# Gate and up in two passes, with 512-column and 256-column matmuls, in a decoder layer in fp32

## The chip, the cores and the metric

The kernel runs on one core of one Trainium2 chip. The metric is the time of one execution on the device, in microseconds (us), as the median of several runs. Engines are named as in the profile: PE is TensorE (PEld its weight loads), DVE is VectorE, ACT is ScalarE, POOL is GpSimd, SP is the engine that issues most DMAs.

## What is computed

One decoder layer on 512 tokens of width 2048 in fp32: a mixer (convolution beside attention), then a gated FFN of width 5632. Only the first half of the FFN is touched:

```python
h = rmsnorm(x, norm2_g[l])
x = x + (jax.nn.silu(h @ w_gate[l]) * (h @ w_up[l])) @ w_down[l]
```

## The kernel before

**Products in three parts.** An fp32 operand is kept as a rounded upper half (hi) and the rest (lo), and a product is three matmuls that accumulate in one PSUM bank: hi x hi, hi x lo, lo x hi. The weights are the stationary operand, the activations the moving one.

**Seven products for eight.** Gate and up take a scheme of the Strassen kind. A block is 256 features of the input by 512 tokens, cut in 2 x 2 quadrants (128 features by 256 tokens); weights are cut in 2 x 2 quadrants of 128 x 128. Seven products of sums of quadrants stand for eight. `block_sums` (L591 on) makes the seven sums of each of the eight blocks (j = 0 to 7) once, with hi in columns 0 to 255 and lo in 256 to 511 of one tile: blocks 0 to 3 in slots b16 to b43, blocks 4 to 7 in slots a0 to a13 and a16 to a29.

**Steps.** The work is a list of steps, one chunk of weights (512 KB) each. In `gu_group` (L661) a step is one block j with 256 columns of gate and the same of up: seven products, each for gate (i = 0) and up (i = 1), of three matmuls of 256 columns (L676 to L678), 42 in all. Eight steps are a pair, 22 pairs make 176 steps. Gate fills columns 0 to 255 and up columns 256 to 511 of a product's bank, seven banks per pair, taken in turn from a ring of eight.

**Splitting a chunk.** `split_gu` (L622) runs two steps ahead, loads run three ahead. The chunk has four quadrants of 256 columns. Three are used as they are, 768 columns: ACT casts them to hi (wh, L638), DVE subtracts to get lo (wl, L649). The four sums are made by DVE (t13, t24: L639, L645, L646), cast by ACT (L647, L648) and subtracted by DVE (L650, L651). raw, wh and wl have three buffers each, t13 and t24 two, their halves three.

**Earlier steps** use another way to get lo, `split_add` (L195): ACT writes the negated hi to wl (L198), and a DMA on POOL's queue adds the weights from memory (L199).

**After a pair** `gu_post` (L683) copies or adds the seven banks into SBUF and puts the remaining sums, the row scale, Silu and the product into a background list, from which each step takes as much as its credit allows. The result, two tiles of hid per pair, goes to memory on POOL's queue (L709).

**Around the stage.** At its entry the last blocks are still being made, and the row scale of the norm (L159, L139, L148, L149) is computed. At its exit `reload_hid` (L741) brings 14 tiles of hid back, on POOL's queue, into the slots of blocks 0 to 3, and `split_hid` makes halves of them; w_down follows, whose first accumulators are banks 0 to 3. A scheduler sets each engine's order from the program and the credits; each engine then works its own instructions in order.

Of the kernel before, what the change touches and what calls it, by code (L numbers as in the profile page):

```python
# [16 lines left out]
P = 128  # L17
S = 512
# [19 lines left out]
STEP_US, GU_STEP_US = 4.6, 5.0  # L38
# [8 lines left out]
def decoder_layer(ctx: ExitStack, tc, xT, w_in, w_out, w_gu, w_dn, par, lamv, out):  # L47
# [543 lines left out]
    def block_sums(j):  # L591
        h = [slotB(44 + i) for i in range(2)]
        for i in range(2):
            kt = 2 * j + i
            nc.scalar.activation(h[i], xres[kt], AF.Copy, scale=pp[:, C_G2 + kt : C_G2 + kt + 1])
        s13, s24 = slotB(46), slotB(47)
        t1, t2 = slice(0, HS), slice(HS, S)
        nc.vector.tensor_tensor(s13[:, t1], h[0][:, t2], h[1][:, t2], op=ALU.add)
        nc.vector.tensor_tensor(s24[:, t1], s13[:, t1], h[0][:, t1], op=ALU.subtract)
        nc.vector.tensor_tensor(s13[:, t2], h[0][:, t2], h[0][:, t1], op=ALU.subtract)  # L600
        nc.vector.tensor_tensor(s24[:, t2], h[1][:, t1], s24[:, t1], op=ALU.subtract)
        forms = [
            h[0][:, t1], h[1][:, t1], s24[:, t2], h[1][:, t2], s13[:, t1], s24[:, t1], s13[:, t2],
        ]
        blocks[j] = []
        for m, f in enumerate(forms):
            t = block_slot(j, m)
            split(t[:, t1], t[:, t2], f)
            blocks[j].append((t[:, t1], t[:, t2]))
# [14 lines left out]
    def split_gu(t, src):  # L624
# [4 lines left out]
        credit[0] -= 3.4  # L629
# [7 lines left out]
        pure = slice(256, 1024)  # L637
        nc.scalar.copy(wh[:, pure], t[:, pure])  # L638
# [10 lines left out]
        nc.vector.tensor_tensor(wl[:, pure], t[:, pure], r32(wh[:, pure]), op=ALU.subtract)  # L649
# [9 lines left out]
    ORDER = [0, 1, 5, 6, 4, 2, 3]  # L659

    def gu_group(pair):  # L661

        accs = {}
        for j in range(NJ):

            def run(q, j=j):
                for n, m in enumerate(ORDER):
                    if j == 0:
                        accs[m] = bank(RING[(7 * pair + n) % 8])
                    sh, sl = blocks[j][m]  # L670
                    qh, ql = q[m]
                    for i in range(2):
                        acc = accs[m][:, i * HS : (i + 1) * HS]
                        cut = slice(i * P, (i + 1) * P)
                        first, last = j == 0 and i == 0, j == NJ - 1 and i == 1
                        nc.tensor.matmul(acc, lhsT=qh[:, cut], rhs=sh, start=first, stop=False)  # L676
                        nc.tensor.matmul(acc, lhsT=qh[:, cut], rhs=sl, start=False, stop=False)  # L677
                        nc.tensor.matmul(acc, lhsT=ql[:, cut], rhs=sh, start=False, stop=last)  # L678

            post = (lambda: gu_post(pair, [accs[m] for m in range(7)])) if j == NJ - 1 else None  # L680
            steps.append((w_gu[pair, j], run, post, split_gu))

    def gu_post(pair, accs):  # L683
        m1, m2, m3, m4, m5, m6, m7 = accs
        tt = nc.vector.tensor_tensor
        u2, c22, v3, v4 = slotA(14, F32), slotA(15, F32), slotA(30, F32), slotA(31, F32)
        c11, u3 = slotB(44), slotB(45)
        nc.scalar.copy(u2, m1)
        tt(c11, m2, u2, op=ALU.add)
        nc.scalar.copy(c22, m5)  # L690
        tt(u2, m6, u2, op=ALU.add)
        nc.scalar.copy(v3, m3)
        tt(u3, m7, u2, op=ALU.add)  # L693
        nc.scalar.copy(v4, m4)
        hid = [slotB(46 + f) for f in range(2)]

        def finish(c, f, i):

            r = rB[1][:, i * HS : (i + 1) * HS]

            def norm():
                c3 = c.rearrange("p (k t) -> p k t", k=2)
                tt(c3, c3, r.unsqueeze(1).to_broadcast([P, 2, HS]), op=ALU.mult)
                nc.scalar.activation(c[:, :HS], c[:, :HS], AF.Silu)

            def product():
                tt(hid[f][:, i * HS : (i + 1) * HS], c[:, :HS], c[:, HS:], op=ALU.mult)
                if i == 1:
                    nc.gpsimd.dma_start(hid_kept[2 * pair + f], hid[f])  # L709

            return norm, product

        n11, p11 = finish(c11, 0, 0)
        n12, p12 = finish(u2, 1, 0)
        n21, p21 = finish(u3, 0, 1)
        n22, p22 = finish(c22, 1, 1)
        bg.extend(
            [
                (0.6, n11),
                (0.6, lambda: tt(u2, u2, c22, op=ALU.add)),  # L720
                (0.6, lambda: tt(c22, u3, c22, op=ALU.add)),
                (0.6, lambda: tt(u2, u2, v3, op=ALU.add)),
                (0.6, lambda: tt(u3, u3, v4, op=ALU.subtract)),
                (0.3, p11),
                (0.6, n12), (0.6, n22), (0.6, n21),
                (0.3, p12), (0.3, p22), (0.3, p21),
            ]
        )
# [61 lines left out]
    for pair in range(NPAIR):  # L790
        gu_group(pair)
# [233 lines left out]
def _layout(i):  # L1025
# [19 lines left out]
    gu = np.stack([f["w_gate"][0], f["w_up"][0]], axis=1).reshape(NJ, 2, P, 2, NPAIR, 2, P)  # L1045
    gu = gu[:, :, :, :, :, ::-1].transpose(4, 0, 2, 1, 5, 3, 6).reshape(NPAIR, NJ, P, 1024)
# [44 lines left out]
```

## Time and profile before

| | us |
|---|---|
| median of 3 runs (2079.77 to 2082.02) | 2081.11 |
| the profiled execution | 2081.82 |
| its span, first to last instruction | 2079.9 |
| PE busy in the span | 2054.6 |
| DVE busy | 1460.8 |
| ACT busy | 942.1 |
| POOL busy | 194.1 |

The mean granted TensorE clock is 0.997 of full speed. Busy times overlap between engines. PE durations overlap too, since matmuls are pipelined: how often they start is read from the timeline. An instruction that issues a DMA is listed with its engine; the transfer itself lands later.

### The profile page before, as it was taken

To read this page: it belongs to the slowest core of one execution; us is meant where nothing else is said; L and a number is where in the kernel's file an instruction comes from. 1 tells how busy PE (TensorE), PEld (TensorE's weight loads), DVE (VectorE), ACT (ScalarE), POOL (GpSimd) and SP (SyncE) were. 2 spreads that over 40 slices of the span, in tenths; PEclk is the share of its full clock that TensorE was granted. 3 is DMA by queue.
4 is the path that set the end of the run, shared out by engine and by line. 5 is a ranking of instruction groups with operands and counts; after the bars stand their busy time and mean duration, and the time that the engine had idled before them with its cause. 6 is when DMAs were issued, how large, how long until landed. Compare 5 with 4: busy or idle time off the path is not lost.

```text
span 2079.9 us, 33053 instructions
## 1 busy us (share of the span) xinstructions
PE 2054.6 (99%) x12852; PEld 1855.1 (89%) x12852; DVE 1460.8 (70%) x2624; ACT 942.1 (45%) x1541; POOL 194.1 (9%) x268
## 2 busy tenths in 40 slices
PE   8999999999999999999999999999999999999997
PEld 6888887888888999999999999999998888888887
DVE  7899935678635899888888988988886333332244
ACT  5433447677744554444444444444444222221232
POOL 5111111111110000000000000000013000000004
PEclk9999999999999999999999999999999999999998
DMA  6888887677763334333333333333358334323232
GB/s 209 186 187 196 191 188 158 149 166 185 181 167 113 122 106 139 112 113 122 122 109 106 132 113 121 120 115 112 113 167 309 102 124 139 98 95 101 92 112 81
DMA packets 84205, 289.74 MB, mean 139 GB/s; under 512 B 10193, under 2 KB 10705, under 8 KB 84049
## 3 DMA queue, kind: packets, MB, share of 16 engines
q1 hardware_dynamic: 61776, 210.04, 30.9%
q0 software_dynamic: 22272, 77.61, 17.3%
q8 instruction: 100, 1.64, 0.3%
q14 instruction: 57, 0.46, 0.1%
HBM read 267.68 MB, written 19.92 MB: 138 GB/s over the span
## 4 chain that ended last, share of the span: by engine, by line
PE 85%; issue 7%; DVE 3%; POOL 1%; ACT 1%; DMA 1%; SPq 0%; DVEq 0%; POOLq 0%; ACTq 0%
PE k L206 14%; PE k L207 14%; PE k L205 14%; PE k L676 14%; PE k L677 14%; PE k L678 14%; POOL wl L199 1%; PE k L519 1%; DMA raw<-w_gu_dram 0%; DVE a L288 0%; PE k L470 0%; DMA wl<-w_v_dram 0%; PE k L469 0%; DVE b L445 0%; PE k L508 0%
## 5 line engine op out<-in xcount | busy, mean ns | idle before, releaser
L205 PE MATMUL k<-a,wh 128*128 128x512 f32 (+1 forms) x992 | 385.4, 389 | 3.2 <-ACT wh L178 1.8
L207 PE MATMUL k<-a,wl 128*128 128x512 f32 (+1 forms) x992 | 383.7, 387 | 2.7 <-DVE wl L179 2.4
L206 PE MATMUL k<-a,wh 128*128 128x512 f32 (+1 forms) x992 | 384.5, 388 | 1.6 <-DVE a L288 1.5
L179 DVE TENSOR_TENSOR wl<-raw,wh 128x1024 fp32r<-128x1024 f32 (+1 forms) x108 | 134.3, 1244 | 319.0 <-ACT wh L178 319.0
L178 ACT CAST wh<-raw 128x1024 fp32r<-128x1024 f32 (+1 forms) x108 | 112.0, 1037 | 365.0 <-PE k L206 355.2
L647 ACT CAST b<-b 128x512 fp32r<-128x512 f32 x176 | 109.2, 621 | 268.4 <-PE k L677 232.1
L205 PEld LDWEIGHTS k<-a,wh 128*128 128x128 f32 x992 | 186.4, 188 | 41.8 <-ACT wh L178 2.4
L207 PEld LDWEIGHTS k<-a,wl 128*128 128x128 f32 x992 | 186.4, 188 | 41.1 <-DVE wl L179 3.7
L206 PEld LDWEIGHTS k<-a,wh 128*128 128x128 f32 x992 | 186.4, 188 | 39.7 <-DVE a L288 2.9
L676 PE MATMUL k<-b,b 128*128 128x256 f32 x704 | 200.2, 284 | 0.9 <-DVE b L693 0.7
L678 PE MATMUL k<-b,b 128*128 128x256 f32 x704 | 199.6, 283 | 0.0
L676 PE MATMUL k<-a,b 128*128 128x256 f32 x704 | 199.2, 283 | 0.0
L677 PE MATMUL k<-a,b 128*128 128x256 f32 x704 | 199.2, 283 | 0.0
L678 PE MATMUL k<-a,b 128*128 128x256 f32 x704 | 199.2, 283 | 0.0
L677 PE MATMUL k<-b,b 128*128 128x256 f32 x704 | 199.2, 283 | 0.0
L335 DVE SCALAR_TENSOR_TENSOR b<-b,pp,b 128x511 f32<-128x511 f32 (+14 forms) x240 | 176.6, 736 | 8.1
L639 DVE TENSOR_TENSOR b<-raw 128x512 f32<-128x512 f32 x176 | 119.7, 689 | 79.8 <-DMA raw<-w_gu_dram 78.6
L205 PE MATMUL k<-b,wh 128*128 128x512 f32 x448 | 174.3, 389 | 0.0
L206 PE MATMUL k<-b,wh 128*128 128x512 f32 x448 | 174.3, 389 | 0.0
L207 PE MATMUL k<-b,wl 128*128 128x512 f32 x448 | 174.3, 389 | 0.0
L649 DVE TENSOR_TENSOR wl<-raw,wh 128x768 fp32r<-128x768 f32 x176 | 167.5, 952 | 0.2 <-ACT wh L638 0.2
L648 ACT CAST b<-b 128x512 fp32r<-128x512 f32 x176 | 109.1, 620 | 120.2 <-DVE b L646 95.8
(212 smaller groups left out, 4961.0 us busy)
## 6 DMA issues: line engine op xcount, KB each, us to landing
raw<-w_gu_dram SPq DMA_DIRECT2D x176, 512.0 KB, 3.3
raw<-w_down_dram SPq DMA_DIRECT2D x88, 512.0 KB, 3.3
raw<-w_qk_dram SPq DMA_DIRECT2D x32, 512.0 KB, 5.5
wl<-w_qk_dram POOLq DMA_DIRECT2D x32, 512.0 KB, 7.4
raw<-w_out_dram SPq DMA_DIRECT2D x32, 512.0 KB, 3.9
raw<-w_conv_dram SPq DMA_DIRECT2D x30, 512.0 KB, 5.2
wl<-w_conv_dram POOLq DMA_DIRECT2D x24, 512.0 KB, 7.7
hid<-b POOLq DMA_DIRECT2D x44, 256.0 KB, 3.3
```

Source lines behind the costliest of these rows:

```text
L178: nc.scalar.copy(hi, src)
L179: nc.vector.tensor_tensor(lo, src, r32(hi), op=ALU.subtract)
L205: nc.tensor.matmul(acc, lhsT=ah, rhs=bh, start=first, stop=False)
L206: nc.tensor.matmul(acc, lhsT=ah, rhs=bl, start=False, stop=False)
L207: nc.tensor.matmul(acc, lhsT=al, rhs=bh, start=False, stop=last)
L335: nc.vector.scalar_tensor_tensor(c[:, d:], h[:, : S - d], w, c[:, d:], op0=ALU.mult, op1=ALU.add)
L639: nc.vector.tensor_tensor(t13.rearrange("p (i c) -> p i c", i=2), t[:, a].unsqueeze(1).to_broadcast([P, 2, 256]), t[:, 256:768].rearrange( ...
L647: nc.scalar.copy(h13, t13)
L649: nc.vector.tensor_tensor(wl[:, pure], t[:, pure], r32(wh[:, pure]), op=ALU.subtract)
L676: nc.tensor.matmul(acc, lhsT=qh[:, cut], rhs=sh, start=first, stop=False)
L677: nc.tensor.matmul(acc, lhsT=qh[:, cut], rhs=sl, start=False, stop=False)
L678: nc.tensor.matmul(acc, lhsT=ql[:, cut], rhs=sh, start=False, stop=last)
```

## The change

Gate and up become separate groups: 44 groups of four steps. A step's chunk now holds two blocks' weights (j = 2 jj and 2 jj + 1) of gate or of up. For each product and block, one matmul of 512 columns multiplies the weights' hi with the block's whole tile, hi and lo, so that the bank's left half gets hi x hi and its right half hi x lo; a second of 256 columns adds lo x hi to the right half. `gu_post` adds the two halves of each bank later. The three plain quadrants get lo by an adding DMA from memory on POOL's queue, after a negation on ACT, in place of DVE's subtraction. The products' order within a step changes, hid goes to memory on SP's queue, and the credits are new. The reloads of hid keep their places in the program.

```diff
-STEP_US, GU_STEP_US = 4.6, 5.0
+STEP_US, GU_STEP_US = 4.6, 4.85
...
-            blocks[j].append((t[:, t1], t[:, t2]))
+            blocks[j].append(t)
...
-        credit[0] -= 3.4
+        credit[0] -= 2.6
...
         pure = slice(256, 1024)
+        nc.scalar.activation(wl[:, pure], t[:, pure], AF.Copy, scale=-1.0)
+        nc.gpsimd.dma_start(wl[:, pure], src[:, pure], accum_op=ALU.add)
         nc.scalar.copy(wh[:, pure], t[:, pure])
...
-        nc.vector.tensor_tensor(wl[:, pure], t[:, pure], r32(wh[:, pure]), op=ALU.subtract)
...
-    ORDER = [0, 1, 5, 6, 4, 2, 3]
-
-    def gu_group(pair):
+    ORDER = [0, 4, 2, 1, 5, 6, 3]
+
+    def gu_group(pair, up):
...
-        for j in range(NJ):
+        for jj in range(NJ // 2):
...
-                    if j == 0:
-                        accs[m] = bank(RING[(7 * pair + n) % 8])
-                    sh, sl = blocks[j][m]
+                    if jj == 0:
+                        accs[m] = bank(RING[(7 * (2 * pair + up) + n) % 8])
                     qh, ql = q[m]
                     for i in range(2):
-                        acc = accs[m][:, i * HS : (i + 1) * HS]
+                        j = 2 * jj + i
                         cut = slice(i * P, (i + 1) * P)
-                        first, last = j == 0 and i == 0, j == NJ - 1 and i == 1
-                        nc.tensor.matmul(acc, lhsT=qh[:, cut], rhs=sh, start=first, stop=False)
-                        nc.tensor.matmul(acc, lhsT=qh[:, cut], rhs=sl, start=False, stop=False)
-                        nc.tensor.matmul(acc, lhsT=ql[:, cut], rhs=sh, start=False, stop=last)
-
-            post = (lambda: gu_post(pair, [accs[m] for m in range(7)])) if j == NJ - 1 else None
-            steps.append((w_gu[pair, j], run, post, split_gu))
+                        nc.tensor.matmul(accs[m], lhsT=qh[:, cut], rhs=blocks[j][m], start=j == 0, stop=False)
+                        nc.tensor.matmul(
+                            accs[m][:, HS:], lhsT=ql[:, cut], rhs=blocks[j][m][:, :HS], start=False, stop=j == NJ - 1
+                        )
+
+            post = (lambda: gu_post(pair, up, [accs[m] for m in range(7)])) if jj == NJ // 2 - 1 else None
+            steps.append((w_gu[pair, up, jj], run, post, split_gu))
...
+    def gu_post(pair, up, accs):
         m1, m2, m3, m4, m5, m6, m7 = accs
+        a, b = slice(0, HS), slice(HS, S)
+        u, c11, u3, v5 = (slotA(n, F32) for n in (14, 15, 30, 31))
+        v3, v4 = slotB(44), slotB(45)
         tt = nc.vector.tensor_tensor
...
+        nc.scalar.copy(u, m1)
+        tt(c11, m2, u, op=ALU.add)
+        nc.scalar.copy(v5, m5)
+        tt(u, m6, u, op=ALU.add)
         nc.scalar.copy(v3, m3)
-        tt(u3, m7, u2, op=ALU.add)
+        tt(u3, m7, u, op=ALU.add)
         nc.scalar.copy(v4, m4)
...
+        outs = [sq_tile(), sum_tile()] if up else [slotB(46), slotB(47)]
+
+        def step(us, *args, op=ALU.add):
+            bg.append((us, lambda: tt(*args, op=op)))
+
+        step(0.34, outs[0][:, a], c11[:, a], c11[:, b])
+        for t in (u, v5, u3):
+            step(0.34, t[:, a], t[:, a], t[:, b])
+        step(0.34, u[:, a], u[:, a], v5[:, a])
+        step(0.34, outs[1][:, b], u3[:, a], v5[:, a])
+        for t in (v3, v4):
+            step(0.34, t[:, a], t[:, a], t[:, b])
+        step(0.34, outs[1][:, a], u[:, a], v3[:, a])
+        step(0.34, outs[0][:, b], u3[:, a], v4[:, a], op=ALU.subtract)
+        for f, c in enumerate(outs):
+            step(0.6, c, c, rB[1], op=ALU.mult)
+            if not up:
+                bg.append((0.0, lambda c=c: nc.scalar.activation(c, c, AF.Silu)))
+                continue
+            step(0.6, c, c, gates[pair][f], op=ALU.mult)
+            bg.append((0.0, lambda c=c, f=f: nc.sync.dma_start(hid_kept[2 * pair + f], c)))
+        if not up:
+            gates[pair] = outs
...
     for pair in range(NPAIR):
-        gu_group(pair)
+        for up in range(2):
+            gu_group(pair, up)
...
-    gu = np.stack([f["w_gate"][0], f["w_up"][0]], axis=1).reshape(NJ, 2, P, 2, NPAIR, 2, P)
-    gu = gu[:, :, :, :, :, ::-1].transpose(4, 0, 2, 1, 5, 3, 6).reshape(NPAIR, NJ, P, 1024)
+    gu = np.stack([f["w_gate"][0], f["w_up"][0]]).reshape(2, NJ // 2, 2, 2, P, NPAIR, 2, P)
+    gu = gu[:, :, :, :, :, :, ::-1].transpose(5, 0, 1, 4, 3, 6, 2, 7).reshape(NPAIR, 2, NJ // 2, P, 1024)
```

The diff does not tell how the scheduler places the new instructions. Three places matter. A row names a line, an operation, what it writes and what it reads; a number behind a name tells tiles of one slot apart, k is a PSUM bank, b and a are SBUF slots.

The first place is TensorE in the middle of the stage: one product of one step, before.

```order
L676 MATMUL k6_9501<-b23_5372,wh_9401 128x256
L677 MATMUL k6_9501<-b23_5372,wh_9401 128x256
L678 MATMUL k6_9501<-b23_5372,wl_9402 128x256
L676 MATMUL k6_9501<-b23_5372,wh_9401 128x256
L677 MATMUL k6_9501<-b23_5372,wh_9401 128x256
L678 MATMUL k6_9501<-b23_5372,wl_9402 128x256
```

And now: one product and a half, where k is the product's bank and the two b tiles are the two blocks.

```order
L676 MATMUL k5_10476<-b31_5585,wh_10372 128x512
L677 MATMUL k5_10476<-b31_5585,wl_10373 128x256
L676 MATMUL k5_10476<-b38_5710,wh_10372 128x512
L677 MATMUL k5_10476<-b38_5710,wl_10373 128x256
L676 MATMUL k6_10481<-b35_5597,b9_10369 128x512
L677 MATMUL k6_10481<-b35_5597,b11_10371 128x256
```

Six matmuls of 256 columns on one block are now four on two blocks, 512 and 256 columns in turn.

The second place is TensorE at the end of the stage's fourth step and the start of the fifth (a11 to a13 and a26 to a29 are block 7; L148 is the product that spreads the row scale).

```order
L676 MATMUL k3_6301<-a12_6476,b5_6311 128x512
L677 MATMUL k3_6301<-a12_6476,b7_6313 128x256
L676 MATMUL k4_6574<-b20_5256,b8_6362 128x512
L148 MATMUL k7_6488<-sq_6407,ones_87 128x512
L676 MATMUL k5_6276<-a13_6479,b4_6310 128x512
L677 MATMUL k5_6276<-a13_6479,b6_6312 128x256
L676 MATMUL k1_6291<-a28_6482,b5_6311 128x512
L677 MATMUL k1_6291<-a28_6482,b7_6313 128x256
L676 MATMUL k2_6296<-a29_6485,b4_6310 128x512
L677 MATMUL k2_6296<-a29_6485,b6_6312 128x256
L676 MATMUL k7_6569<-b16_5244,wh_6366 128x512
```

Block 7's last three products stand at the very end of the fourth step, behind L148 and behind one matmul of the fifth; before, block 7 was not used until the eighth step. The bank k7 of L148 is taken next by the fifth step's first product.

The third place is POOL's queue at the end of the stage, before: stores of hid and reloads of hid in turn, no weights.

```order
L709 DMA hid38_166<-b46_16859 128x512
L741 DMA b17_17495<-hid0_128 128x512
L741 DMA b21_17501<-hid2_130 128x512
L741 DMA b19_17498<-hid1_129 128x512
L741 DMA b23_17565<-hid3_131 128x512
L709 DMA hid41_169<-b47_17388 128x512
L709 DMA hid40_168<-b46_17387 128x512
L741 DMA b27_17571<-hid5_133 128x512
```

And now (wl_16206 is the chunk of the second-last step of the stage, wl_16279 that of the last):

```order
L639 DMA wl_16206<-w_gu_dram 128x768
L735 DMA b23_16072<-hid3_131 128x512
L735 DMA b27_16078<-hid5_133 128x512
L735 DMA b25_16075<-hid4_132 128x512
...
L735 DMA b33_16135<-hid8_136 128x512
L735 DMA b41_16230<-hid12_140 128x512
L735 DMA b43_16233<-hid13_141 128x512
L639 DMA wl_16279<-w_gu_dram 128x768
```

All 14 reloads stand between the last two adding transfers of the stage.

## Rows read from the trace of the kernel before

**Rows 1.** The page, part 1: busy us, share of the span, instructions.

```profile
PE 2054.6 (99%) x12852; PEld 1855.1 (89%) x12852; DVE 1460.8 (70%) x2624; ACT 942.1 (45%) x1541; POOL 194.1 (9%) x268
```

**Rows 2.** The page, part 4: the chain that ended last, shares by engine.

```profile
PE 85%; issue 7%; DVE 3%; POOL 1%; ACT 1%; DMA 1%; SPq 0%; DVEq 0%; POOLq 0%; ACTq 0%
```

**Rows 3.** Windows: length, busy us and instructions, granted clock, DMA share, GB/s.

```profile
core 0: us, PE busy (x) PEld busy (x) DVE busy (x) ACT busy (x) POOL busy (x), PEclk, DMA share, GB/s
100.00:150.00 50.00, 50.00 (x223) 41.40 (x222) 47.21 (x68) 20.12 (x22) 7.50 (x10) 1.00 0.88 191
1000.00:1050.00 50.00, 50.00 (x419) 50.00 (x419) 41.79 (x73) 23.05 (x38) 1.07 (x2) 1.00 0.33 106
689.60:1581.43 891.83, 890.94 (x7403) 888.79 (x7402) 791.80 (x1409) 433.21 (x729) 39.91 (x75) 1.00 0.38 125
```

**Rows 4.** Timeline of PE, 256 columns: start us, us, instruction.

```profile
1551.79 0.28 PE L678 MATMUL k<-b,wl 128*128 128x256 f32 x1
...
1558.63 0.28 PE L678 MATMUL k<-b,b 128*128 128x256 f32 x1
```

**Rows 5.** Timeline of PE, 512 columns, in w_down.

```profile
1599.82 0.39 PE L205 MATMUL k<-b,wh 128*128 128x512 f32 x1
...
1611.83 0.39 PE L207 MATMUL k<-b,wl 128*128 128x512 f32 x1
```

**Rows 6.** Timeline of PE, both widths, in the attention stage.

```profile
329.81 0.40 PE L206 MATMUL k<-a,wh 128*128 128x512 f32 x1
330.04 0.28 PE L470 MATMUL k<-b,b 128*128 128x256 f32 x1
330.16 0.39 PE L207 MATMUL k<-a,wl 128*128 128x512 f32 x1
```

**Rows 7.** Groups of 700 to 1450 us, by form: busy us, mean ns | idle before.

```profile
L638 ACT CAST wh<-raw 128x768 fp32r<-128x768 f32 x148 | 123.4, 834 | 13.5 <-PE k L677 4.2 <-issue 3.0 <-PE k L678 0.4
L647 ACT CAST b<-b 128x512 fp32r<-128x512 f32 x149 | 92.5, 621 | 239.2 <-PE k L677 213.1 <-DVE b L639 20.7 <-issue 5.2
L688 ACT COPY a<-k 128x512 f32<-128x512 f32 x18 | 10.6, 587 | 2.7 <-PE k L678 2.7
```

**Rows 8.** Timeline of DVE where it runs without a gap.

```profile
1026.18 0.95 DVE L649 TENSOR_TENSOR wl<-raw,wh 128x768 fp32r<-128x768 f32 x1
1027.05 0.42 DVE L645 TENSOR_TENSOR b<-raw,b 128x256 f32<-128x256 f32 x1
1027.38 0.69 DVE L650 TENSOR_TENSOR b<-b,b 128x512 fp32r<-128x512 f32 x1
1027.98 0.42 DVE L646 TENSOR_TENSOR b<-b,raw 128x256 f32<-128x256 f32 x1
```

**Rows 9.** Instructions on the tile wl: ns min/median/max, first and last start.

```profile
L198 ACT ACTIVATE wl<-raw x88: 1045/1055/1065, 47.5 to 587.2; 128x1024 fp32r<-128x1024 f32 x88
L199 POOL DMA_DIRECT2D wl<-w_conv_dram x24: 854/863/1047, 48.9 to 176.4; - x24
...
DMA to landing us min/median/max: 5.4/7.7/9.7
```

**Rows 10.** Line L199: who waited for its 88 adding transfers (us, times).

```profile
  PEld k L206: 1.2, 2
  PEld k L207: 0.9, 2
  PE k L206: 0.6, 1
  PE k L207: 0.3, 1
```

**Rows 11.** Timeline of DVE: after the last w_out product, and block 7's end.

```profile
686.24 0.68 DVE L572 TENSOR_TENSOR b<-k,b 128x512 f32<-128x512 f32 x1
...
710.06 1.76 DVE L179 TENSOR_TENSOR a<-b,a 128x256 fp32r<-128x256 f32 x5
```

**Rows 12.** Groups of POOL: the reloads of hid.

```profile
L741 POOL DMA_DIRECT2D b<-hid x28 | 15.0, 539 | 161.9 <-PE k L206 123.1 <-PE k L678 34.9 <-issue 2.4
```

More of the change, by code (lines that the diff above doesn't have):

```diff
@@ L658, in decoder_layer, with run @@
     RING = [4, 5, 6, 0, 1, 2, 3, 7]
-    ORDER = [0, 1, 5, 6, 4, 2, 3]
-    def gu_group(pair):
+    ORDER = [0, 4, 2, 1, 5, 6, 3]
+    def gu_group(pair, up):
         accs = {}
-        for j in range(NJ):
-            def run(q, j=j):
+        for jj in range(NJ // 2):
+            def run(q, jj=jj):
                 for n, m in enumerate(ORDER):
-                    if j == 0:
-                        accs[m] = bank(RING[(7 * pair + n) % 8])
-                    sh, sl = blocks[j][m]
+                    if jj == 0:
+                        accs[m] = bank(RING[(7 * (2 * pair + up) + n) % 8])
@@ L678, in run @@
-                        nc.tensor.matmul(acc, lhsT=ql[:, cut], rhs=sh, start=False, stop=last)
-            post = (lambda: gu_post(pair, [accs[m] for m in range(7)])) if j == NJ - 1 else None
-            steps.append((w_gu[pair, j], run, post, split_gu))
-    def gu_post(pair, accs):
+                        nc.tensor.matmul(accs[m], lhsT=qh[:, cut], rhs=blocks[j][m], start=j == 0, stop=False)
+                        nc.tensor.matmul(
+                            accs[m][:, HS:], lhsT=ql[:, cut], rhs=blocks[j][m][:, :HS], start=False, stop=j == NJ - 1
+                        )
@@ L684, in gu_post @@
+            post = (lambda: gu_post(pair, up, [accs[m] for m in range(7)])) if jj == NJ // 2 - 1 else None
+            steps.append((w_gu[pair, up, jj], run, post, split_gu))
+    gates = {}
+    def gu_post(pair, up, accs):
         m1, m2, m3, m4, m5, m6, m7 = accs
+        a, b = slice(0, HS), slice(HS, S)
+        u, c11, u3, v5 = (slotA(n, F32) for n in (14, 15, 30, 31))
+        v3, v4 = slotB(44), slotB(45)
         tt = nc.vector.tensor_tensor
-        u2, c22, v3, v4 = slotA(14, F32), slotA(15, F32), slotA(30, F32), slotA(31, F32)
@@ L687, in gu_post @@
[L687 to L691, printed above, removed]
+        nc.scalar.copy(u, m1)
+        tt(c11, m2, u, op=ALU.add)
+        nc.scalar.copy(v5, m5)
+        tt(u, m6, u, op=ALU.add)
         nc.scalar.copy(v3, m3)
-        tt(u3, m7, u2, op=ALU.add)
+        tt(u3, m7, u, op=ALU.add)
         nc.scalar.copy(v4, m4)
[L695 to L728, printed above, removed]
+        outs = [sq_tile(), sum_tile()] if up else [slotB(46), slotB(47)]
```

## The prediction

> **What bounds the kernel now.** I read the page first, then the chain of waits, then stretches of the windows view, then single rows of the timeline. The page says that TensorE is busy 99% of the span and VectorE 70% [rows 1]; the chain that ended last runs through TensorE for 85% [rows 2]. Those shares are averages over stages, so the stage of the change decides: from 689.60 to 1581.43 us, 891.83 us in all, TensorE is busy for 890.94 at granted clock 1.00 and starts 7403 matmuls, while VectorE is busy for 791.80, ScalarE for 433.21, and DMA for 0.38 [rows 3]. 7392 of those matmuls are gate and up: 176 steps of 42. Nothing else limits here, so what counts is how often a matmul can start.
>
> The timeline gives that. A row's own duration (0.28 or 0.39 us) overlaps with the next, so starts are compared. The 256-column matmuls start every 120.0 ns (57 intervals in 6.84 us, [rows 4]). The 512-column ones of w_down start every 226.6 ns (53 intervals in 12.01 us, [rows 5]). Twice the columns cost 106.6 ns more, which is 256 columns at 2.4 GHz; so each matmul pays about 13.4 ns beside its columns. Where the attention stage puts one 256-column matmul among 512-column ones, the starts go 329.81, 330.04, 330.16: 0.23, then 0.12 [rows 6]. The mixture costs the sum of its parts.
>
> **The change, part by part.** *Matmuls.* A step has seven products of two sets each; the three 256-column matmuls of a set become one of 512 and one of 256, the same 768 columns. Before 3 x 120.0 = 360.0 ns, after 226.6 + 120.0 = 346.6. That is 14 sets a step, 176 x 14 = 2464 in the stage: 887.0 us before, 854.0 after, **33.0 us less**. A step takes 5.04 us before and 4.85 after. All of it is on the path.
>
> The Trainium skill, page "TensorE: Matmul & The Clock Gate", section "Back-to-back issue gap", has N/2.4 + 2.5 ns for a warm matmul. By it a saved matmul is worth an estimated 2.5 ns and this part 6.2 us, not 33.0. The trace disagrees: it has 120.0 where that gives 109 and 226.6 where that gives 216, so I take the measured spacing.
>
> *VectorE.* The 768-column subtraction goes; each group of four steps instead adds halves. Work costs its distance between starts: 768 columns 0.87, 256 columns 0.33, 512 columns 0.60 us [rows 8]. After, a step has 3 x 0.60 + 2 x 0.33 = 2.46, and a group 3 x 0.60 + 10 x 0.33 and two (gate) or four (up) of 0.60, so 6.3 or 7.5, 1.7 per step: 4.2 of 4.85 us. Before it was 2.46 + 0.87 + (11 x 0.60 + 4 x 0.33)/8 = 4.3 of 5.04. The share stays at 86%; TensorE covers it, and splits are made two steps ahead, so I cost it at nothing. Were VectorE the bound, a step would still be 4.2, under 4.85.
>
> *ScalarE.* The negation is new: 768 columns, between the 834 ns of the cast of the same tile [rows 7] and the 1055 ns of the 1024-column negation [rows 9]; I take 0.84, the same width. Per step 2 x 0.84 + 2 x 0.62, and per group four copies of 0.59 and half of two 512-column Silus at about 0.62 (as the 512-column cast): (2.92 + 0.75) = 3.7 of 4.85 us. Covered, but it is now ahead of a transfer.
>
> *The adding transfer.* Each step sends 384 KB more through the POOL queue. Path: the buffer of chunk s+3 is chunk s's, and its last reader is the fourth of seven products, 4/7 x 4.85 = 2.77 us into step s. Then cast 0.84 and negation 0.84, in order on ScalarE, then issue to landing 7.7 us (5.4 to 9.7 over 88 transfers of 512 KB [rows 9]): 12.2 us. It is wanted when step s+3 begins, 14.56 us. Spare: 2.4 us, 0.4 at the slowest landing. Nothing shows 384 KB alone; the bounds are 5.4 and 9.7, and I take 7.7, though the transfer is smaller. In stages that already do this, with a step of 5.44 us (24 matmuls), TensorE waited 1.2 + 0.9 + 0.6 + 0.3 = 3.0 us for all 88 [rows 10]. The load on DMA will be like theirs: 106 GB/s now [rows 3] x 5.04/4.85 + 393216 B/4.85 us = 191 GB/s, and 191 GB/s is what 100 to 150 us shows, at DMA share 0.88 with no stall on TensorE [rows 3]. So nothing in the steady part.
>
> *hid to the SP queue.* It leaves POOL's queue, where it would stand among adding transfers, and now has weight loads behind it. For a group whose last step is s, the store comes ready after some 6 us of VectorE work, in step s+1, and by the instruction order the load behind it is chunk s+8's: nothing.
>
> *Entry.* Two blocks of the left factor are now used per step, so block 7 is wanted in the fourth step, not the eighth. VectorE finished block 7 at 710.06 + 1.76 = 711.8, having worked from 686.24 on [rows 11]; the fourth step now runs from 689.60 + 3 x 4.85 = 704.2 to 709.0. The order puts block 7's last three products and the product for the row scale at its end, so if the blocks came as late as before, those 3 x 0.35 us would start at 711.8: 712.9 in place of 709.0, a stall of 3.9. Four subtractions of 0.87 fewer lie on VectorE's way by then: as little as 0. More transfers and the bank of the row scale are also late there. I take 3, bounds 0 and 5.
>
> *Exit.* Here the order says more than the diff. The 14 reloads of hid take the slots of blocks 0 to 3, which are now read in the first two steps of the last group, and the last chunk's adding transfer stands behind all 14 on POOL. With S the start of that group's second step, the reload that waits longest wants block 2's part of the seventh product, done at 6/7 x 4.85 + 0.35 = S + 4.5; it and two more, issued in 0.54 each [rows 12], bring the transfer to S + 6.1, and it lands 7.7 later, S + 13.8. The last step wants it at S + 2 x 4.85 = S + 9.7: **a stall of 4.1**, bounds 1.8 (landing 5.4) and 6.1 (9.7). Then w_down's first accumulator takes bank 0, which the last product now leaves last: one copy of 0.59 [rows 7], with its signals about 1. I take 5 for the exit, bounds 2 and 8.
>
> Sum, against the profiled execution: 2081.8 - 33.0 + 3 + 5 = 2056.8. The median of the three runs is 0.7 below that execution, so **2056 us**; with the bounds 2050 to 2061.
>
> **Rivals.** *A, the boundaries hide:* landing at 5.4 and block 7 in time leave 0 to 2 us: 2048 to 2050. For it: transfers are smaller than those measured. Against: the exit's queue is plain.
>
> *B, a stall per group:* 44 times, after the last step of a group, ScalarE has four copies around the cast and negation. If the three of 0.59 that stand ahead push them by 1.8 us, the spare of 2.4 holds at the median landing but not at 9.7, where 1.4 is missing; in between, 0.1 to 0.5 a group makes 4 to 22 us: 2060 to 2078. Against: those three banks are done at 0.7, 1.4 and 2.1 us of the step, before the cast may begin.
>
> *C, the adding transfer becomes the bound (slower):* the buffer cycle is 2.43 steps long and holds 1.7 us plus the landing L, so a step cannot be shorter than (1.7 + L)/2.43. It equals 4.85 at L = 10.1 and the old 5.04 at 10.6; at L = 11 a step is 5.22, 176 of them 919 us against 887, and the time 2081 + 32 + 8 = 2121. With the boundaries counted the change turns slower from L = 10.5 on. For it: raw loads, adding transfers and hid share the engines and POOL issues beside a VectorE that is busy 86%. Against: no landing above 9.7 in 88, where VectorE was busy 47.21 of 50 us [rows 3], and issue took 863 ns at the median, 1047 at most [rows 9]. The Trainium skill, page "SBUF — State Buffer", section "SBUF: two separate sides", says that GpSimd cannot write descriptors while VectorE holds the shared ports in a two-port mode; by it such transfers would start late, and the issue rows do not show it.
>
> *D, the saved matmuls give nothing:* if the 13 ns belonged to the change of shape, a set would cost 360 ns again, and with the boundaries the time is 2081 + 8 = 2089. [Rows 6] speak against it (0.35, not 0.36, though a row resolves only 0.01). The formula of the Trainium skill above (TensorE page) is its milder form: only 6.2 of the 33.0 us come, 2083 by estimate.
>
> **How the numbers follow.** Forecast 0.74, A 0.08, B 0.10, C 0.06, D 0.02. No change means within 0.2%, about what a measurement of this kernel can tell: 4.2 us, 2077 to 2085. Forecast, A and most of B are faster: 0.90. A fifth of B and a sixth of C stay within: 0.03. The rest of C and D are slower: 0.07. The range takes in forecast and A, with a microsecond below, and most of B: 2047 to 2070.
>
> **What would show it.** Right: in the steady part, starts 0.23 and 0.12 apart, a stage of 854 to 865 us, DMA near 0.85 and 190 GB/s, ScalarE near 75%; one TensorE wait of 2 to 6 us for a transfer into wl at the start of the stage's last step, one of about 1 us for a copy at the first w_down matmul, some small ones within 25 us of the entry. Wrong: TensorE waits for wl transfers spread over the stage (B: every fourth step; C: every step, with landings above 10 us), or sets 0.36 us long (D). If VectorE rather than DMA ends TensorE's waits in the steady part, my cover for the added sums was wrong.

## The result, and the profile after

Predicted were 2056 us, range 2047 to 2070. The changed kernel took 2052.44 us in the median of four runs (2050.22, 2052.12, 2052.76, 2070.3) against 2080.44 for the kernel before beside it: 0.988 of it, 95% interval 0.984 to 0.993. The profiled execution took 2052.76 us, 29.1 less than that of before. In six more runs three were near 2052 and three near 2066, so nine of ten lie in the range; what sets the two levels apart is told below.

The page, parts 1 and 4, against [rows 1, 2]:

```profile
PE 2023.1 (99%) x10388; PEld 1718.4 (84%) x10388; DVE 1436.8 (70%) x2822; ACT 1118.8 (55%) x1761; POOL 322.4 (16%) x400
PE 92%; issue 3%; DVE 2%; ACT 1%; DMA 1%; POOL 0%; SPq 0%; DVEq 0%; POOLq 0%; ACTq 0%
```

TensorE is the bound as before, with 2464 matmuls fewer. The windows view gives the stage (first row), a steady part, and two stretches at its end; columns as in [rows 3]:

```profile
689.77:1554.36 864.59, 859.22 (x4940) 750.14 (x4938) 771.22 (x1609) 610.31 (x950) 163.68 (x199) 1.00 0.90 208
1000.00:1500.00 500.00, 500.00 (x2883) 436.83 (x2882) 447.67 (x931) 350.74 (x542) 89.03 (x103) 1.00 0.90 204
1535.00:1543.50 8.50, 8.50 (x49) 7.17 (x47) 6.97 (x12) 6.50 (x11) 5.16 (x10) 1.00 1.03 393
1547.98:1552.19 4.21, 4.21 (x13) 3.63 (x14) 2.66 (x5) 2.83 (x6) 0.54 (x1) 0.50 1.02 406
```

The stage of 891.83 us [rows 3] takes 864.59, 27.2 less. In 500 us of its middle TensorE is always busy. The waits of its matmuls in the whole stage are two, by the waits view (us in total, times, longest):

```profile
PE k L677 <- DMA wl<-w_gu_dram: 4.5, 1, 4.5
PE k L676 <- ACT a L178: 0.9, 1, 0.9
```

From 715 to 1540 us two weight loads wait besides, at 1453.69 and 1454.62, for sums on VectorE that read their banks. They cost 0.6 us together:

```profile
PEld k L676 <- DVE a L695: 0.3, 1, 0.3
PEld k L676 <- DVE a L697: 0.3, 1, 0.3
```

The first of the matmuls' waits is the stall at the exit. TensorE's timeline there shows a second cost behind it:

```profile
1542.78 0.39 PE L676 MATMUL k<-a,wh 128*128 128x512 f32 x1
1543.01 0.39 PE L676 MATMUL k<-a,b 128*128 128x512 f32 x1
1543.24 0.28 PE L677 MATMUL k<-a,b 128*128 128x256 f32 x1
1547.98 0.58 PE L677 MATMUL k<-a,wl 128*128 128x256 f32 x1 [4.46 <-DMA wl<-w_gu_dram]
1548.35 0.63 PE L676 MATMUL k<-a,wh 128*128 128x512 f32 x1
1548.78 0.41 PE L677 MATMUL k<-a,wl 128*128 128x256 f32 x1
1548.99 0.63 PE L676 MATMUL k<-a,b 128*128 128x512 f32 x1
...
1551.98 0.41 PE L677 MATMUL k<-a,wl 128*128 128x256 f32 x1
1552.19 0.47 PE L676 MATMUL k<-a,b 128*128 128x512 f32 x1
```

The start that was due at 1543.36 comes at 1547.98, 4.62 later. Then a set takes 0.64 us (1548.35 to 1548.99) instead of 0.347, until 1552.19: the last window above shows granted clock 0.50 there, the lower level of 1.2 GHz; TensorE had stood idle for 4.5 us ahead of it, and the clock was 1.00 before. Six sets and a short matmul cost 4.21 us in place of 2.2, so the stall costs 2.0 us more after it is over. Together 6.6.

Why the transfer is late stands in GpSimd's timeline:

```profile
1528.14 0.86 POOL L639 DMA_DIRECT2D wl<-w_gu_dram  x1 [3.99 <-ACT wl L638]
1530.05 2.70 POOL L735 DMA_DIRECT2D b<-hid  x5 [1.05 <-PE k L677]
...
1538.32 0.54 POOL L735 DMA_DIRECT2D b<-hid  x1 [0.61 <-PE k L677]
1539.56 0.54 POOL L735 DMA_DIRECT2D b<-hid  x1 [0.69 <-DMA raw<-w_down_dram]
1540.67 0.54 POOL L735 DMA_DIRECT2D b<-hid  x1 [0.58 <-DMA b<-hid]
1542.10 0.89 POOL L639 DMA_DIRECT2D wl<-w_gu_dram  x1 [0.89 <-ACT b L740]
```

Its negation was done at 1532.7; it is issued at 1542.10, behind the 14 reloads, one of which waits for the seventh product (1538.32) and the next two, by the view, until other transfers have landed. The last 0.89 us ahead of it the view puts down to a cast of hid on ScalarE, which it doesn't need; what it waited for there stays open. It lands 5.9 later.

Groups of steps give the account. By TensorE's timeline a group of eight steps took 40.32 us before, and a group of four takes 19.41 now, 4.853 a step. What comes on top: in the first 42 us 1.9 before and 3.1 now; at group changes 2.9 before (six of them, 0.2 to 1.0 each) and 0.6 now (one); in the last group 0 before and 6.7 now. So 22 x 40.32 + 4.8 = 891.8 before, and 44 x 19.413 + 10.4 = 864.6 now.

### The profile page after: what moved, and what is told of

Read it like the earlier page. It is cut to its first block, busy times and chain, and to the rows that moved or that the text cites. A ratio compares the mean times of both kernels' runs of the same rounds, so it can differ in the third digit from the quotient of the medians.

```text
span 2051.0 us, 28884 instructions
## 1 busy us (share of the span) xinstructions
PE 2023.1 (99%) x10388; PEld 1718.4 (84%) x10388; DVE 1436.8 (70%) x2822; ACT 1118.8 (55%) x1761; POOL 322.4 (16%) x400
## 4 chain that ended last, share of the span: by engine, by line
PE 92%; issue 3%; DVE 2%; ACT 1%; DMA 1%; POOL 0%; SPq 0%; DVEq 0%; POOLq 0%; ACTq 0%
PE k L676 27%; PE k L207 16%; PE k L205 16%; PE k L206 16%; PE k L677 13%; PE k L519 1%; DVE a L288 0%; PE k L470 0%; PE k L469 0%; DVE b L445 0%; PE k L508 0%; DMA b<-hid 0%; DMA x<-b 0%; DMA wl<-w_gu_dram 0%; DMA raw<-w_conv_dram 0%
## 5 line engine op out<-in xcount | busy, mean ns | idle before, releaser
L639 POOL DMA_DIRECT2D wl<-w_gu_dram x176 | 152.2, 865 | 725.7 <-ACT wl L638 700.2
L640 ACT CAST wh<-raw 128x768 fp32r<-128x768 f32 x176 | 147.1, 836 | 196.1 <-PE k L676 108.6
L676 PE MATMUL k<-a,b 128*128 128x512 f32 x704 | 252.8, 394 | 0.0
L676 PE MATMUL k<-b,b 128*128 128x512 f32 x704 | 252.5, 394 | 0.0
L677 PE MATMUL k<-a,b 128*128 128x256 f32 x704 | 195.2, 277 | 0.0
L677 PE MATMUL k<-b,b 128*128 128x256 f32 x704 | 195.1, 277 | 0.0
L676 PE MATMUL k<-a,wh 128*128 128x512 f32 x528 | 192.7, 396 | 0.9 <-ACT a L178 0.9
L676 PE MATMUL k<-b,wh 128*128 128x512 f32 x528 | 191.1, 394 | 0.0
L206 PE MATMUL k<-b,wh 128*128 128x512 f32 x448 | 174.3, 389 | 0.0
L205 PE MATMUL k<-b,wh 128*128 128x512 f32 x448 | 174.1, 389 | 0.0
L200 ACT CAST wh<-raw 128x1024 fp32r<-128x1024 f32 x88 | 92.0, 1045 | 136.6 <-issue 77.3
L676 PEld LDWEIGHTS k<-a,b 128*128 128x128 f32 x704 | 132.3, 188 | 30.8 <-DVE a L179 0.2
```

The costliest lines, as they stand in the source:

```text
L200: nc.scalar.copy(wh, t)
L205: nc.tensor.matmul(acc, lhsT=ah, rhs=bh, start=first, stop=False)
L206: nc.tensor.matmul(acc, lhsT=ah, rhs=bl, start=False, stop=False)
L639: nc.gpsimd.dma_start(wl[:, pure], src[:, pure], accum_op=ALU.add)
L676: nc.tensor.matmul(accs[m], lhsT=qh[:, cut], rhs=blocks[j][m], start=j == 0, stop=False)
L677: nc.tensor.matmul(accs[m][:, HS:], lhsT=ql[:, cut], rhs=blocks[j][m][:, :HS], start=False, stop=j == NJ - 1)
```

## The experiments

**The same kernel again**, without an edit; the run at 2070.3 asked for it.

> The changed kernel once more, unaltered. One of its four runs took 2070.3, the others 2050.2 to 2052.8. Theory (a single disturbed execution): all new runs lie within 2049 to 2054. Rival (a second level of the kernel itself, as of a transfer that comes late in some executions): at least one more run near 2070.

Six runs: 2050.5, 2051.96, 2052.65, 2065.28, 2065.47, 2066.94; ratio to before 0.989 (0.986 to 0.992). The rival holds, but not by a late transfer: the profiled run was a long one (2066.94), and the waits of TensorE's matmuls are those of the quick one (1.3 and 4.1 us here, 0.9 and 4.5 there). What differs is the pace. Adding transfers go out once a step; 20 steps in the quick execution (first fence) and in the long one:

```profile
804.45 0.86 POOL L639 DMA_DIRECT2D wl<-w_gu_dram  x1 [3.98 <-ACT wl L638]
...
901.51 0.86 POOL L639 DMA_DIRECT2D wl<-w_gu_dram  x1 [3.99 <-ACT wl L638]
```

```profile
799.82 0.87 POOL L639 DMA_DIRECT2D wl<-w_gu_dram  x1 [4.09 <-ACT wl L638]
...
898.74 0.86 POOL L639 DMA_DIRECT2D wl<-w_gu_dram  x1 [4.08 <-ACT wl L638]
```

97.06 / 20 = 4.853 us a step against 98.92 / 20 = 4.946: 346.7 against 353.3 ns a set, with granted clock 1.00 in both. The long execution keeps its pace in every stretch of 25 us from 725 to the exit, whatever the other engines do; its stage takes 880.7 us, 16.1 more, and 2464 sets at 6.7 ns make 16.4. I call the two paces the quick and the slow rhythm.

**Three short matmuls again.**

```diff
-nc.tensor.matmul(accs[m], lhsT=qh[:, cut], rhs=blocks[j][m], start=j == 0, stop=False)
+for x in (slice(0, HS), slice(HS, S)):
+    nc.tensor.matmul(
+        accs[m][:, x], lhsT=qh[:, cut], rhs=blocks[j][m][:, x],
+        start=j == 0 and x.start == 0, stop=False,
+    )
```

> The changed kernel with three matmuls of 256 columns again in each set instead of one of 512 and one of 256; groups, layout, adding transfers and summing of halves stay. Theory (the whole gain is the 13.4 ns that a matmul pays beside its columns): a step is 5.04 us again, the stage 33 us longer, 2084 to 2087, so slower than before the change by 3 to 6 us. Rival (the gain comes from the new groups and from work taken off VectorE): within 5 us of the changed kernel, 2050 to 2058.

2083.59 (2082.58 to 2087.75, ten runs), 0.4 under the range of the theory and 1.0014 of before (1.0005 to 1.0022): the gain is the merged matmuls and nothing else pays. Without them the rest of the change makes the kernel slightly slower than before. The steady part holds 4169 matmuls in 500 us, one every 120 ns, as before the change:

```profile
1000.00:1500.00 500.00, 500.00 (x4169) 500.00 (x4168) 437.04 (x895) 337.91 (x522) 85.59 (x99) 1.00 0.86 196
```

**All lower halves on VectorE.**

```diff
-nc.scalar.activation(wl[:, pure], t[:, pure], AF.Copy, scale=-1.0)
-nc.gpsimd.dma_start(wl[:, pure], src[:, pure], accum_op=ALU.add)
+nc.vector.tensor_tensor(wl[:, pure], t[:, pure], r32(wh[:, pure]), op=ALU.subtract)
```

> The changed kernel with every pure lower half subtracted on VectorE again: no negation on ScalarE, no adding transfer. Theory (the transfers are what makes room on VectorE): VectorE is busy 447.67 of 500 us in the steady part, 4.34 of a step of 4.85; with 0.87 more it needs 5.1 to 5.2, becomes the bound and TensorE waits for it: 44 to 61 us more, 2090 to 2115, slower than before the change; DMA share falls to about 0.35. Rival (VectorE's busy time overlaps and its queue runs ahead far enough): no bound, 2044 to 2053, as fast as the changed kernel or faster by the exit's stall.

2091.24 (2090.83 to 2092.17), 1.005 of before (1.003 to 1.006): slower than before. VectorE is full and TensorE waits on what it feeds; window and waits of this kernel:

```profile
1000.00:1500.00 500.00, 489.68 (x2748) 416.49 (x2747) 499.43 (x985) 254.02 (x414) 0.00 (x0) 1.00 0.36 116
```

```profile
PE k L675 <- ACT b L647: 11.4, 19, 4.3
PE k L676 <- DVE wl L649: 8.7, 20, 0.8
```

So each half of the change needs the other: the adding transfers give nothing by themselves, but pay for VectorE's room.

**Two wl buffers.**

```diff
+if c == 0:
+    held.append(wts.tile([P, 1024], F32R, tag="wl", bufs=3, name="held"))
+    nc.vector.memset(r32(held[0][:, :1]), 0.0)
...
+if c == 175:
+    nc.vector.tensor_copy(t13[:, :1], r32(held[0][:, :1]))
```

> The changed kernel with one of the three wl buffers held empty through the whole stage, so that chunk s+2 takes chunk s's. Theory (the cycle of the prediction: a step cannot be shorter than (1.7 + L)/1.43 with two buffers, L from issue to landing): with L 6.4 as the median now a step is 5.7 us, 176 of them 145 us more than 4.86, 2200; with L down to 5.4 in the thinner traffic 5.0, 2075. So 2075 to 2200, TensorE waiting for wl in every step. Rival (the third buffer is not what gives the cover, the scheduled order of the engines is): 2050 to 2067 as the changed kernel.

2161.36 (2159.71 and 2163.0); TensorE waits for wl 86 times, 77.0 us, in about every second step and not in every one, and a step takes 5.49 us on average. Landing was 5.9 at the median there, so the cycle gives (1.7 + 5.9) / 1.43 = 5.31, 3% short of it. The formula of the prediction holds that nearly; with three buffers it allows 3.3 us at the changed kernel's landing, and the step of 4.85 lies well clear.

**A wider transfer.**

```diff
-nc.scalar.activation(wl[:, pure], t[:, pure], AF.Copy, scale=-1.0)
-nc.gpsimd.dma_start(wl[:, pure], src[:, pure], accum_op=ALU.add)
+nc.scalar.activation(wl, t, AF.Copy, scale=-1.0)
+nc.gpsimd.dma_start(wl, src, accum_op=ALU.add)
```

> The changed kernel with negation and adding transfer of all 1024 columns of a chunk, 512 KB in place of 384; the 256 columns more are not used. Theory (DMA is the next bound and the margin is small): a plain 512 KB load takes 0.33 of a step of 5.04 us of the 16 engines before the change, 1.66 us; the changed kernel uses 0.89 of 4.86, 4.3 us, so 384 KB of adding take about 2.4 and 512 KB 3.2; with hid's stores a step needs 5.0 to 5.1 us of DMA: TensorE waits for wl in every step, landings go above 10 us, and the time is 2078 to 2095. Rival (an adding transfer costs by the number of its rows, not by their length): share and landing stay, 2050 to 2067, the levels of the changed kernel.

A miss: 2068.61 (2062.32 to 2074.97). The share rises to 0.96 only, landing is 7.7 at the median and 9.4 at most, and apart from the exit TensorE waits for wl once (0.6 us). 128 KB more cost 0.96 x 4.95 - 0.90 x 4.86 = 0.4 us of DMA a step, half of what I had worked out from the 384 KB. Neither theory fits: by this estimate the longer adding transfer costs less than in proportion to its length, and not nothing. What stretches this run is mostly the rhythm again, slow for most of the stage, and here it changes within one execution.

**Exit: the last chunk on VectorE.**

```diff
-nc.scalar.activation(wl[:, pure], t[:, pure], AF.Copy, scale=-1.0)
-nc.gpsimd.dma_start(wl[:, pure], src[:, pure], accum_op=ALU.add)
+if c < 175:
+    nc.scalar.activation(wl[:, pure], t[:, pure], AF.Copy, scale=-1.0)
+    nc.gpsimd.dma_start(wl[:, pure], src[:, pure], accum_op=ALU.add)
+if c == 175:
+    nc.vector.tensor_tensor(wl[:, pure], t[:, pure], r32(wh[:, pure]), op=ALU.subtract)
```

> The last chunk of the gate-up stage alone gets its pure lower half by a VectorE subtraction, as all chunks did before the change; no adding transfer stands behind the 14 reloads of hid any more. Theory (the queue order on GpSimd makes the stall, and the stall makes the low clock behind it): the 4.5 us wait at 1543 goes, and so do the 4.2 us at granted clock 0.50 after it, in which the work takes 2.0 us longer than at full clock: 6.6 us less, about 2046 against 2052.8 of the profiled execution; no TensorE wait for wl in the stage and clock 1.00 from 1535 to 1560. Rival (the 16 DMA engines are full there, share 1.03): the wait comes back for raw or hid at the first w_down matmuls, 2049 to 2053. Second rival (the clock falls for another reason): only 4.6 go, 2048, and the half clock stays.

2050.64 (2049.09 to 2051.53), 0.985 of before (0.984 to 0.986), only 1.4 below the quick level of the changed kernel (2052.0). The stall at 1543 is gone, and the clock is 1.00 there; so the queue made the one and the stall the other. But w_down's first accumulation on bank 0 now meets a copy that stands on ScalarE behind casts of hid, three other copies and a cast of w_down's weights, and behind that wait the clock falls as before (waits, then the window after it, in which 0.50 until 1555.02 and 0.92 from there make 0.60):

```profile
PE k L205 <- ACT b L701: 3.2, 1, 3.2
```

```profile
1551.86:1556.00 4.14, 4.14 (x11) 3.32 (x12) 4.14 (x12) 0.00 (x0) 2.66 (x5) 0.60 1.03 394
```

**Exit: and another bank first.**

```diff
-at[d0].append(lambda: homes.update(t=[6, 7]))
+at[d0].append(lambda: (homes.update(t=[6, 7]), turn.update(mm=1)))
```

> As e1_exit, and w_down's four accumulators start with bank 1 instead of bank 0. In e1_exit the stall moved to the first w_down matmuls (3.2 us for the copy of bank 0, which ScalarE makes last, behind casts of hid) and the clock fell behind it again. Theory (the stall is the order of the banks; banks 1, 2, 3 come free earlier): at most 1 us of wait at w_down's entry, clock 1.00 there, 2045 to 2047 where gate and up run at 346.7 ns a set. Rival (the full DMA engines, share 1.0 from 1535 to 1560, hold the entry whatever the banks): the wait comes back for hid or raw, 2049 to 2052 as e1_exit.

2045.18 (2044.29 to 2045.47), 0.9825 of before (0.981 to 0.984) and 6.9 below the quick level of the changed kernel, where 6.6 were to be had. At DMA share 1.03 TensorE is busy for 24.95 of 25 us and the clock stays at 1.00:

```profile
1535.00:1560.00 25.00, 24.95 (x127) 20.91 (x126) 22.25 (x37) 14.60 (x23) 16.41 (x31) 1.00 1.03 389
```

So full DMA engines were not the cause. The same kernel once more:

> The kernel of e5_bank once more. Its four runs lay within 2044.3 to 2045.5, all in the quick rhythm (346.7 ns a set), and so did the four of e1_exit, while four of ten of the changed kernel lay some 14 us higher. Theory (the rhythm is set by the short waits at the stage's entry, which these kernels share with the changed one): the slow level comes here too, in two to four of ten, at 2059 to 2062. Rival (the edits at the exit took the slow level away): all runs again within 2044 to 2046.

2044.4, 2045.02, 2046.72, 2047.52 and 2060.48: the slow rhythm comes here too (the profiled run is the long one), in one of nine runs, so the rival is out. The theory is half right: here the rhythm turned slow at 754.5, behind the entry (last section). Rhythm for rhythm this version beats the changed kernel, 2045 and 2060 us against 2052 and 2066.

**Long, long, short, short.**

```diff
-for i in range(2):
-    j = 2 * jj + i
-    cut = slice(i * P, (i + 1) * P)
+cuts = [(2 * jj + i, slice(i * P, (i + 1) * P)) for i in range(2)]
+for j, cut in cuts:
     nc.tensor.matmul(accs[m], lhsT=qh[:, cut], rhs=blocks[j][m], start=j == 0, stop=False)
+for j, cut in cuts:
     nc.tensor.matmul(
...
```

> The changed kernel with the four matmuls of a product in the order long, long, short, short instead of long, short, long, short; the work is the same. In two executions of the changed kernel the sets ran at 346.7 and at 353.4 ns through the whole stage, constant in every 25 us and without a wait; 2464 sets make 16.5 us of it, the distance of the two levels of its times. Theory (the slow rhythm belongs to the alternation of long and short matmuls, each short one standing under a weight load of a long one): with pairs a product takes 693 ns in every run, and all runs lie within 2050 to 2054. Rival (the slow rhythm comes from the execution, not from the order): again two levels some 14 us apart. Second rival (a long matmul behind a long one and a short behind a short one cost more or less than 226.6 and 120.0): one level elsewhere, 3 us for every 0.6 ns a matmul.

2056.45 (2054.09 to 2056.85). A step takes 4.877 us, 348.3 ns a set: one level, as the second rival had it, 1.6 ns above the quick rhythm; a product takes 697 ns and not 693. The same edit together with the two at the exit:

> The kernel of e5_bank with the matmuls of a product in pairs, long, long, short, short. In e6_pairs a step took 4.877 us in place of 4.853 (348.3 ns a set) and the four runs lay in one level. Theory (pairs have one rhythm, a little slower): 2464 sets at 1.6 ns more make 3.9 us, 2048 to 2050 in all runs. Rival (pairs have a slow rhythm too, not met in four runs): some runs 10 us or more above.

2050.57 (2049.12 to 2051.89). Eight runs of pairs show no slow level; among the kernels with long and short in turn (leaving out the wide transfer and the two buffers) it held seven of 27 runs, so eight without one is suggestive and not proof. The two profiled runs of pairs also had none of the short hold-ups at which the others changed pace (last section). Pairs lose to alternation as long as the slow rhythm is rarer than one run in four (3.9 against 16.4 us); at seven of 27 the two are about even.

**The old order of products.**

```diff
-ORDER = [0, 4, 2, 1, 5, 6, 3]
+ORDER = [0, 1, 5, 6, 4, 2, 3]
```

> The changed kernel with the order of products from before the change: the wl buffer is read last by the sixth of seven products instead of the fourth, so its transfer starts 2/7 of a step, 1.39 us, later. By the trace of the changed kernel a transfer is issued 4.8 us into step s, lands 6.4 later at the median and 9.8 at most, and is wanted 14.8 us after the step's start: spare 3.6 at the median, 0.2 at the slowest. Theory: spare 2.2 and -1.2, so TensorE waits for wl in a few steps, 0 to 4 us in the stage, 2050 to 2056 in the quick rhythm and 14 more in the slow one. Rival (the new order is what keeps the transfers in time): waits for wl spread over the stage, above 2070.

2070.45 (2068.34 and 2072.56). Apart from the exit TensorE's matmuls wait for wl twice, 1.2 and 0.9 us, so the spare was read rightly; the rest is the slow rhythm, from 736.40 on, where a weight load waited 0.26 us for wl. The time alone fits both (14 more in the slow rhythm is 2064 to 2070, the rival had above 2070); the waits decide, since they are not spread over the stage. The second wait shows what it hangs on. GpSimd's adding transfers ahead of it (16 steps) and behind it (8), and between them TensorE's row:

```profile
1332.99 0.86 POOL L639 DMA_DIRECT2D wl<-w_gu_dram  x1 [4.04 <-ACT wl L638]
...
1412.13 0.87 POOL L639 DMA_DIRECT2D wl<-w_gu_dram  x1 [4.03 <-ACT wl L638]
...
1457.51 0.87 POOL L639 DMA_DIRECT2D wl<-w_gu_dram  x1 [3.99 <-ACT wl L638]
...
1496.34 0.86 POOL L639 DMA_DIRECT2D wl<-w_gu_dram  x1 [3.99 <-ACT wl L638]
```

```profile
1440.51 0.40 PE L676 MATMUL k<-a,wh 128*128 128x512 f32 x1
1441.76 0.38 PE L677 MATMUL k<-a,wl 128*128 128x256 f32 x1 [0.85 <-DMA wl<-w_gu_dram]
```

79.14 / 16 = 4.946 us a step ahead, 38.83 / 8 = 4.854 behind. The rhythm changed at a short wait, and to the quick one. The wait of 1.2 us at 806 had left it slow.

**Stores of hid on GpSimd.**

```diff
-nc.sync.dma_start(hid_kept[2 * pair + f], c)
+nc.gpsimd.dma_start(hid_kept[2 * pair + f], c)
```

> The changed kernel with the stores of hid on GpSimd's queue again. By the order of instructions both stores of a pair stand behind the transfer of the fifth chunk after the group's last step begins; by the trace that transfer is issued 9.6 us after that step's start, the products are done at 11.7 and the next transfer is due at 14.5, so the stores fit between. Theory: no difference, 2050 to 2053 in the quick rhythm or 14 more in the slow one, TensorE's waits the same. Rival (the stores hold up the transfers behind them, and the move to the other queue is a needed part of the change): a wait for wl at each of 22 pairs, 1 to 4 us each, 2075 to 2140.

2050.68 (2050.52 and 2050.83): no difference. The stores go out at 1009.3 and 1009.9, between transfers at 1007.6 and 1012.5.

## Why the prediction was right, and where it was not

**Matmuls, -33.0: right in the quick rhythm.** A step takes 4.853 us where 4.852 was worked out, and 44 x 19.413 against 22 x 40.32 is 32.9 less. The three-matmul kernel gives it back. The sum of the parts, not the formula of the Trainium skill (page "TensorE: Matmul & The Clock Gate", section "Back-to-back issue gap"), was the one to take: by that formula 6 us would have come, by estimate. That section of the Trainium skill gives the formula for an isolated matmul and says that in a stream the weight loads set the spacing too, which the prediction left out. What the step missed is that the same mixture has a second price. In the slow rhythm a set costs 353.3 ns and half of the 13.4 ns is lost, a mild form of rival D, in four of ten runs; [rows 6] resolve 10 ns and could not show 6.7.

**VectorE and ScalarE: right.** 447.67 of 500 us is 90% where I had 86, ScalarE 70% where I had 75, and no matmul in the steady part waits for either. The two weight loads that wait 0.3 us each for VectorE cost 0.6 us, so the cover is thin; the all-VectorE kernel shows that it was as thin as the sum said.

**The adding transfer: right, its landing too long.** I took 7.7 from transfers of 512 KB; the 384 KB ones take 6.4 at the median, 4.8 to 9.8. The one for a chunk is issued 4.8 us into a step (1003.43, the step having begun at 998.66), 0.3 later than worked out, so the spare is 3.4 us and not 2.4. Rows of this stage:

```profile
L639 POOL DMA_DIRECT2D wl<-w_gu_dram x176: 854/863/894, 680.8 to 1542.1; - x176
DMA to landing us min/median/max: 4.8/6.4/9.8
```

No transfer passed the limit of rival C, and rival B's waits at group changes did not come. On the contrary, 2.3 us at group changes are gone, which I had not counted.

**Entry, 3: too much.** 1.2 us more than before. The one wait of a matmul listed, 0.9 us at 707.40, ends on ScalarE's cast of a block, not on VectorE's last subtraction for block 7.

**Exit, 5: right by terms that were not.** Predicted was a stall of 4.1 and about 1 for bank 0. The start came 4.6 late, but out of other parts: the last group's second step began at 1533.07, and the transfer left 9.0 us later, not 6.1, since the reload that waits for the seventh product was issued 0.7 later than worked out, and the two behind it and the transfer itself waited 0.7, 0.6 and 0.9 more; it landed in 5.9 and not 7.7; and three matmuls that don't need it, 0.6 us, stand ahead. Bank 0 cost next to nothing: four matmuls that don't need it stand ahead, and ScalarE, which had cleared its casts during the stall, copied it from 1554.56 on, right behind the last product. Without the stall (kernel with the last chunk on VectorE) the same copy starts 3.7 us behind the start of the stage's last matmul and costs 3.2. The 2.0 us at half clock were not in the sum. That the 6.7 us lie within the bounds of 2 to 8 is in part luck.

The sum as measured: -32.9 for matmuls, -2.3 at group changes, +1.2 at the entry, +6.7 in the last group, is -27.3, and the stage shows -27.2. Another 1.8 us are saved outside the stage, 1.5 of them behind the kernel's last matmul, on instructions that the change does not touch; runs of one kernel differ by as much.

## What to carry to other kernels

Count the matmuls, not the columns, as long as the spacing in the trace shows a fixed part beside the columns, and pay for merging with whatever engine has room: neither half of this change is worth anything alone. Ask of each transfer that is new on a queue what stands ahead of it at the stage's last step; and price a stall of TensorE with the slow clock behind it. Time a kernel often enough to see whether it has two levels, and look for the pace of the steady part before looking for waits; where the pace changes, look at the waits of weight loads too.

## What the runs showed of the hardware that was not expected

**Two rhythms.** Alternating 512- and 256-column matmuls settle at 346.7 or 353.3 ns a set and keep it for hundreds of us without a wait. The pace changes where TensorE is held up briefly, in either direction: from slow to quick at 1441.76 above, and from quick to slow in the wide-transfer kernel at 1331.08, where the next start comes 0.1 us late (346.7 ns a set from 1275 to 1325, 353.4 from 1350 on):

```profile
1330.86 0.28 PE L677 MATMUL k<-b,b 128*128 128x256 f32 x1
1331.08 0.50 PE L676 MATMUL k<-b,b 128*128 128x512 f32 x1
1331.42 0.28 PE L677 MATMUL k<-b,b 128*128 128x256 f32 x1
```

No matmul's wait is listed there, but the weight load at 1331.08 waited 0.26 us for VectorE's sum of the group before. One kernel shows it in both rhythms: of the two profiled runs of the kernel with another bank first, the quick one had two such waits (first fence; 753.59 and 754.53) and stayed at 346.7; the long one had only the second (754.53, with the two matmuls behind it), ran at 346.7 before and at 353.3 from there to the exit:

```profile
PEld k L679 <- DVE a L700: 0.3, 1, 0.3
PEld k L679 <- DVE a L698: 0.2, 1, 0.2
```

```profile
PEld k L679 <- DVE a L700: 0.2, 1, 0.2
754.53 0.50 PE L679 MATMUL k<-b,b 128*128 128x512 f32 x1
754.86 0.28 PE L680 MATMUL k<-b,b 128*128 128x256 f32 x1
```

In such a hold-up the short matmul starts 0.34 us behind the long one, where 0.23 is the rule. In the profiled runs with long and short in turn (leaving out the all-VectorE and the two-buffer kernel, which wait all the time), a single one behind the entry turned the quick rhythm slow four times of four: also in the wide-transfer kernel at 815.41, and with the old order at 736.40, there for a transfer into wl. Two of them 0.9 us apart left it quick three times of three: also in the changed kernel at 1453.69 and 1454.62, and in the wide-transfer kernel at 756.11 and 757.04. So did five in 2.4 us at 1270 in the wide-transfer kernel, and a smaller one (0.30 us, 1519.30, old order); two single ones in the slow rhythm left that slow (754.02 and 766.14, old order). In the long run of the changed kernel the pace is slow from the entry on, where several waits stand close together; which of them set it can't be read. What in TensorE holds the rhythm stays open, as does why one hold-up changes it and two do not. Between hold-ups it doesn't move with what DMA or the other engines do.

**The clock behind a stall.** After idle stretches of 4.5 and 3.2 us the granted clock was 0.50 for the next 4.2 and 3.2 us of the rows, though TensorE worked without a gap.
